# End of the first block's attention: a norm weight as a column, the pool mixer's two halves back to back, w_out's upper parts on ScalarE

## The chip, the cores and the metric

The kernel runs on one core of one Trainium2 chip. The metric is the device time of one execution in microseconds; below it is the median of the executions shown.

## What is computed

Two transformer blocks follow each other on 256 tokens of 1024 numbers, in float32. The change touches the end of the mixer of the first block. That mixer projects the normalized input and feeds three branches: a gated delta rule with 6 heads, an attention with compressed, selected and windowed keys, and a pool mixer that subtracts a token from running means over 2, 4, 8 and 16 tokens. The three outputs stand beside each other (384, 384 and 256 columns), and one product brings them back into the residual:

```python
o = gated_delta_rule(q, k, v, beta, g)
o = rms_norm(o, norm_g) * jax.nn.silu(heads(z))          # delta rule's output
mean = (cg[:, 1:] - cg_lag) / jnp.minimum(t1, float(w))  # pool mixer, per window w
outs.append(jnp.einsum('btc,cd->btd', mean - uf[..., sl], pool_w[gi]))
y = jnp.concatenate([y_a, y_b, y_c], axis=-1)
x = x + y @ w_out[l]
```

`norm_g` has 64 numbers, one for each place in a head, the same for all heads. After that come a feed-forward part, the second block with two attentions, and a layer of 32 experts, which this kernel goes through one after the other.

## The kernel before, in words

Activations stand in two layouts: tokens on the 128 partitions (two tiles `t` of 128 tokens) or channels on the partitions (`yT`, `xT`, 8 chunks of 128 channels by 256 tokens). For products in full precision each operand is split into an upper and a lower part, and three matmuls are made (`mm3`, L302 to L304; `mmc`, L404 to L406). A weight is split by `split` (L287 to 299): the upper part by an ACTIVATE on ScalarE (L297) or a TENSOR_SCALAR on GpSimd (L295), the lower part by a subtraction on VectorE (L298). With no engine named, `split` takes turns between ScalarE and GpSimd. There are three buffers for each part, so an upper part can be made only when the matmuls of the third one before it are done.

`block1` writes its steps as Python generators and calls them in the order of a string written out by hand, `ORDER1`. It sets the priority of every instruction. The order on each engine's queue is then made by a planner, which runs the program against its own costs of the instructions and issues what is ready in its model, by priority. On the chip each queue runs in that order, and an instruction that must wait holds up everything behind it on its engine.

The steps that matter here:

- `z` (`w_z`, L538 to 553) projects the gate z and applies silu to it, on token tiles. Its matmuls are the last that read `xT1`, whose two buffers `y_tiles` then hands to `yT`.
- `pm` (`pool_mix`, L667 to 697) has two halves `a`, and gives control back after each. For each it makes the running sums on GpSimd (L683 to 689), one pair of matmuls for each of two heads into a bank of PSUM (L693), and evicts the bank to the upper part of `yT` on ScalarE (L694) and the lower part on VectorE (L695).
- `rec` (`recur` and `out`) ends with the delta rule's output `y_a` of token tile t: sum with the last product (L1268), squares and their sum (L1270, L1272, L1273), the inverse root on GpSimd (L312, called with the name `rO`), and the product with it (L1276).
- `fin` (`finish`, L1278 to 1294) multiplies z by the norm weight on GpSimd (L1284), then y by z on VectorE (L1285), transposes y on TensorE in three pairs of heads (L1291, two PSUM banks in turn) and evicts each to `yT` (L1293 on ScalarE, L1294 on VectorE).
- `no` (`Nsa.out`, L898 to 944) makes the scores against the compressed keys (L910, L916), their softmax on VectorE and ScalarE (L921 to L929), transposes it (L933), evicts it (L935), multiplies with the values (L941), adds (L942) and writes chunks 3 to 5 of `yT` (L943, L944).
- `o` (`w_out`, L562 to 576) loads w_out, and multiplies for each half of the 1024 output columns the chunks of `yT` in the order 6, 7, 0, 1, 2, 3, 4, 5. Each chunk is one split and six matmuls (128x512). The loads go through SyncE's queue into a ring of six buffers of 1 MB.

The expert weights (some 200 MB) pass through the same queue and stream from HBM to the end of the program.

Of the kernel before, what the change touches and what calls it, by code (L numbers as in the profile page):

```python
# [9 lines left out]
F32 = mybir.dt.float32  # L10
# [3 lines left out]
AF = mybir.ActivationFunctionType  # L14
OP = mybir.AluOpType
# [3 lines left out]
P = 128  # L19
# [6 lines left out]
BK = dict(k="acc", v="acc", q="acc", nq="acc", ks="mg", kc="acc", u="mn", z="acc", a0="mn", a1="acc", a2="mn", a3="acc", a4="mn", a5="acc")  # L26
ORDER1 = ("nq k k gates k k nq gates k nq low v nq nq ks ks ks nq low kc ks ks low ks np v np v np v v v dbl "
# [3 lines left out]
SPL2 = dict(fq="p", fk="a", fv="g", dq="g", dk=None, dv=None, g0="g", g1="a", g2="g", g3="a", pa="a", pb=None, o0=None, o1=None, o2=None)  # L31
BK2 = dict(fq="acc", fk="acc", fv="acc", dq="acc", dk="acc", dv="acc", g0="acc", g1="acc", g2="acc", g3="acc")
ORDER2 = ("fk x x fq fk fk fk fk lam fq fq fv fq fq fq x fg fg fk fv fv fv fv fv dk f1 dk f1 f2 dk f1 dq f2 "
# [15 lines left out]
def _pack(items, dtype=np.float64):  # L49
    off, arrs, o = {}, [], 0  # L50
    for name, a in items:
        a = np.asarray(a, dtype).reshape(P, -1)
        off[name] = (o, a.shape[1])
        arrs.append(a)
        o += a.shape[1]
    return off, np.concatenate(arrs, axis=1)
# [52 lines left out]
def _params(I):  # L109

    def row(a):
        a = np.asarray(a).reshape(1, -1)
        return np.broadcast_to(a, (P, a.shape[1]))

    cw = I["conv_w"][0]
    first = [("g_mix", I["norm_mix"].reshape(8, P).T),
             ("cwT", cw.T.reshape(9, P, 4).transpose(1, 0, 2)),
             ("alog", row(I["a_log"])),
             ("dtb", row(I["dt_bias"])),
             ("wba", np.concatenate([I["w_in"][0][:, 1536:1548], I["w_in"][0][:, 2700:2718]], 1)  # L120
              .reshape(8, P, 30).transpose(1, 0, 2))]
    kn = I["nsa_k_norm"][0]
    rest = [("gng", row(I["gdn_norm"])),
            ("qcol", np.tile(I["nsa_q_norm"][0], 2)),
            ("kcol", np.tile(kn.T, (2, 1))),
            ("krow", row(kn[0])),
            ("posT", I["cmp_pos"][0].reshape(2, 16, 2, 64).transpose(2, 3, 0, 1)),
            ("w2c", I["cmp_w2"][0].reshape(2, 2, P, 64).transpose(2, 0, 1, 3)),
            ("pw", I["pool_w"][0].reshape(2, 2, 64, 64).transpose(1, 2, 0, 3)),
            ("psc", I["pool_scale"].reshape(2, P).T)]  # L130
    wr = np.concatenate([I["w_group_2"][0], I["w_expert_2"][0]], 1)
    dense = [("g_ffn", I["norm_ffn"].reshape(8, P).T)]
    block2 = [("g_mix2", I["g_mix_2"].reshape(8, P).T),
              ("bfg", row(I["b_fgate_2"])),
              ("lq", np.concatenate([row(I[n]) for n in ("lam_q1_2", "lam_q2_2", "lam_k1_2", "lam_k2_2")], 1)),
              ("gsub", I["g_subln_2"].reshape(P, 1)),
              ("wff", I["w_in_2"][0][:, 1536:1544].reshape(8, P, 8).transpose(1, 0, 2)),
              ("g_moeT", I["g_moe_2"].reshape(8, P).T),
              ("wr", wr.reshape(8, P, 36).transpose(1, 0, 2)),
              ("br", np.concatenate([row(I["b_group_2"]), row(I["b_expert_2"])], 1))]  # L140
    moe = [("g_moe", I["g_moe_2"].reshape(P, 8))]
    return [_pack(i, np.float32) for i in (first, rest, moe, block2, dense)]


_P1_SHAPES = (("g_mix", 8), ("cwT", 36), ("alog", 6), ("dtb", 6), ("wba", 240))
_P2_SHAPES = (("gng", 64), ("qcol", 1), ("kcol", 3), ("krow", 64), ("posT", 32), ("w2c", 256), ("pw", 128), ("psc", 2))
_P3_SHAPES = (("g_moe", 8),)
_P4_SHAPES = (("g_mix2", 8), ("bfg", 8), ("lq", 256), ("gsub", 1), ("wff", 64), ("g_moeT", 8), ("wr", 288), ("br", 36))
_P5_SHAPES = (("g_ffn", 8),)
# [287 lines left out]
def block1(K):  # L437
    nc, tc, I = K.nc, K.tc, K.I
    V, S, G, PE = K.V, K.S, K.G, K.PE
    C, CB, PR, idn, idb, mg, acc, dump = K.C, K.CB, K.PR, K.idn, K.idb, K.mg, K.acc, K.dump  # L440
    xt = K.xt
    with ExitStack() as st1:
        sp = K.sp
# [86 lines left out]
        z = wk.tile([P, 2, 384], F32, name="z")  # L530
# [22 lines left out]
        yT = []  # L553
# [6 lines left out]
        wo = []  # L560

        def w_out():  # L562
            for k in range(2):
                wo.append(load_out(K, I["w_out"][0][:, k * 512:k * 512 + 512], f"w_out{k}"))
                yield
            st1.close()
            K.early.close()
            s8b = K.st8.enter_context(tc.tile_pool(name="s8b", bufs=1, reuse_waits="tile"))
            K.s8b = lambda dt, name: s8b.tile([P, 8, T], dt, name=name, tag="s8b", bufs=2)
            K.xf = K.Rows(xt, PR("g_ffn"), "xTf", (K.s8b, K.s8b))  # L570
            for k in range(2):
                def ev(t, pv):
                    xs = xt[:, t, k * 512:k * 512 + 512]
                    V.tensor_tensor(xs, pv, xs, op=OP.add)
                yield from K.lin_tok(yT, wo[k], 512, sp, ev, order=(6, 7, 0, 1, 2, 3, 4, 5))
                K.xf.half(k)

        steps = dict(k=w_k(), v=w_v(), q=w_q(), nq=w_nq(), ks=w_ks(), kc=w_kc(), u=w_u(), z=w_z(), y=y_tiles(), o=w_out(),
# [1 line left out]
                     rec=g.recur(), fin=g.finish(z, yT), np=n.prep(few[:, :, 12:30]), cmp=n.compress(rbc),  # L580
                     no=n.out(yT), pm=pool_mix(K, wk, uT, yT))
# [365 lines left out]
def bc(ap, shape, axis):  # L947

    ix = [slice(None)] * len(ap.shape)
    ix.insert(axis, None)  # L950
    return ap[tuple(ix)].to_broadcast(list(shape))
# [13 lines left out]
class Gdn:  # L965
# [312 lines left out]
    def finish(self, z, yT):  # L1278
        K, wk, y = self.K, self.wk, self.y
        V, S, G, PE, mg, idn = K.V, K.S, K.G, K.PE, K.mg, K.idn  # L1280
        H = 6
        for t in range(2):
            zv = z[:, t].rearrange("p (h d) -> p h d", h=H)
            G.tensor_tensor(zv, zv, bc(K.PR("gng"), (P, H, 64), 1), op=OP.mult)  # L1284
            V.tensor_tensor(y[:, t], y[:, t], zv, op=OP.mult)  # L1285
            yield
        K.dump("y_a", y)
        for a in range(3):
            py = mg((P, 2, P), name="py")
            for t in range(2):  # L1290
                PE.transpose(py[:, t], y[:, t, 2 * a:2 * a + 2].rearrange("p a b -> p (a b)"), idn)  # L1291
            pf = py.rearrange("p a b -> p (a b)")
            S.activation(yT[0][:, a], pf, AF.Copy)  # L1293
            V.tensor_tensor(yT[1][:, a], pf, yT[0][:, a].bitcast(F32), op=OP.subtract)  # L1294


def attn_probs(K, wk, sc, off, nk, tag):
# [817 lines left out]
def device_arrays(inputs):  # L2115
    import ml_dtypes
    arrays = {f"in_{n}_dram": np.ascontiguousarray(inputs[n]) for n in _INS}
    arrays["in_c0_dram"] = _C0.astype(np.float32)
    arrays["in_cf_dram"] = _CF.astype(np.float32)
    arrays["in_cd_dram"] = _CD.astype(np.float32)  # L2120
    arrays["in_cb_dram"] = _CB.astype(ml_dtypes.bfloat16)
    arrays["in_cm_dram"] = _CM.astype(np.float32)
    arrays["in_cu_dram"] = _CU.astype(ml_dtypes.bfloat16)
    for n, (_, a) in zip(("p1", "p2", "p3", "p4", "p5"), _params(inputs)):
        arrays[f"in_{n}_dram"] = np.ascontiguousarray(a, np.float32)
    return arrays
# [15 lines left out]
```

## Time and profile before

| what | value |
| --- | --- |
| median of 3 runs | 1039.4 us (1038.61 to 1040.7) |
| the profiled execution | 1036.04 us, its span 1034.1 us |
| TensorE busy with matmuls | 989.6 us, 96% of the span |
| VectorE, ScalarE, GpSimd busy | 461.6, 277.3, 228.9 us |
| mean granted TensorE clock | 0.990 of full speed |

The span runs from the first to the last instruction in the profile; all times of a row are microseconds from its start. Matmuls are pipelined, so the profile's duration of one is longer than the distance to the next. PE is TensorE, DVE is VectorE, ACT is ScalarE, POOL is GpSimd, SP is SyncE. A row's bracket gives the time in which the engine stood idle before the instruction and what ended that wait.

### The profile page before, as it was taken

The numbers are of one execution on the slowest core, as the hardware profiler recorded it, in microseconds if no ns is written. First come the engines' busy times: TensorE is split into PE (matmuls) and PEld (weight loads), VectorE is DVE, ScalarE is ACT, GpSimd is POOL, SyncE is SP. The second block draws the span as 40 slices with busy tenths as digits, with TensorE's granted clock in tenths as the row PEclk, the third lists the DMA queues.
The fourth block names the chain that finished last, engine by engine and source line by source line (L and its number), as shares of the span: only waits on it lengthen the run. The fifth ranks groups of instructions, "written<-read, shape, count | busy, mean of one in ns | idle before, by whom it ended". The sixth has DMA issues, their size and how long they took to land. (4 is left out here: it accounts for less than half of the span.)

```text
span 1034.1 us, 16556 instructions
## 1 busy us (share of the span) xinstructions
PE 989.6 (96%) x6613; PEld 686.2 (66%) x6613; DVE 461.6 (45%) x948; ACT 277.3 (27%) x635; POOL 228.9 (22%) x318
## 2 busy tenths in 40 slices
PE   7999988999999999999999899999999999999995
PEld 6778766899988888887788434444444555555352
DVE  3878866665566653567688511111111111111012
ACT  3543333433333342435343011111101111111012
POOL 3682442222222225443337400000000000000000
PEclk9999997999999999999999999999999999999998
DMA  9552363755555554365677799999999999999994
GB/s 345 146 167 94 107 182 129 282 176 191 184 189 198 177 170 153 123 204 175 222 259 312 272 394 421 420 419 420 421 421 418 421 420 421 419 419 420 420 410 179
DMA packets 81999, 292.61 MB, mean 283 GB/s; under 512 B 11584, under 2 KB 26240, under 8 KB 58880
## 3 DMA queue, kind: packets, MB, share of 16 engines
q1 hardware_dynamic: 80768, 289.68, 73.9%
q10 hardware_dynamic: 1152, 1.86, 0.5%
q8 instruction: 53, 0.87, 0.3%
q14 instruction: 26, 0.21, 0.1%
HBM read 289.87 MB, written 1.64 MB: 282 GB/s over the span
## 5 line engine op out<-in xcount | busy, mean ns | idle before, releaser
L1802 PE MATMUL ph<-w,xe 128*64 128x512 f32 x1024 | 227.0, 593 | 2.3 <-DMA w<-in_w_dram 2.3
L1802 PEld LDWEIGHTS ph<-w,xe 128*64 128x64 f32 x1024 | 85.5, 137 | 132.5 <-issue 124.7
L1802 PE MATMUL po_e<-w,gT 128*64 128x512 f32 x528 | 115.1, 584 | 0.7 <-ACT gT L1911 0.7
L298 DVE TENSOR_TENSOR wl<-ffn,wh 128x512 fp32r<-128x512 f32 (+1 forms) x100 | 84.6, 849 | 62.4 <-ACT wh L297 31.3
L312 POOL TENSOR_TENSOR r<-r4a,mhalf 128x2 f32<-128x2 f32 x1 | 0.7, 698 | 442.1 <-DVE r4a L310 442.1
L1896 DVE COPY ws<-ppt 64x2 f32<-64x2 f32 x32 | 5.0, 157 | 194.8 <-ACT pT L1893 194.6
L1802 PEld LDWEIGHTS po_e<-w,gT 128*64 128x64 f32 x528 | 40.1, 136 | 63.8 <-issue 55.9
L295 POOL TENSOR_SCALAR wh<-ffn 128x512 fp32r<-128x512 f32 (+1 forms) x50 | 44.5, 890 | 138.3 <-PE acc_c L405 61.1
L405 PE MATMUL acc_c<-xTfl,wh 128*128 128x256 f32 x256 | 70.2, 283 | 0.0
L404 PE MATMUL acc_c<-xTfh,wh 128*128 128x256 f32 x256 | 70.1, 283 | 0.0
L1893 ACT ACTIVATE pT<-ppt 128x256 fp32r<-128x256 f32 x16 | 6.1, 384 | 225.4 <-PE ppt L1802 225.4
L406 PE MATMUL acc_c<-xTfh,wl 128*128 128x256 f32 x256 | 64.6, 283 | 0.0
L297 ACT ACTIVATE wh<-ffn 128x512 fp32r<-128x512 f32 (+1 forms) x50 | 37.4, 751 | 84.9 <-PE acc_c L405 42.2
L303 PE MATMUL acc<-wl,hh 128*128 128x512 f32 x128 | 50.8, 397 | 0.0
L304 PE MATMUL acc<-wh,hl 128*128 128x512 f32 x128 | 50.6, 395 | 0.0
L405 PEld LDWEIGHTS acc_c<-xTfl,wh 128*128 128x128 f32 x256 | 49.0, 192 | 0.5
L404 PEld LDWEIGHTS acc_c<-xTfh,wh 128*128 128x128 f32 x256 | 48.8, 192 | 0.4
L1802 PE MATMUL pgat<-ohb,xp 128*128 128x128 bf16 x768 | 48.4, 219 | 0.5 <-DVE ohb L1815 0.5
L1802 PEld LDWEIGHTS <-xp 128*128 128x128 bf16 x768 | 44.5, 98 | 6.3 <-issue 6.1
L406 PEld LDWEIGHTS acc_c<-xTfh,wl 128*128 128x128 f32 x256 | 45.6, 192 | 0.1
L303 PE MATMUL acc_t<-wl,xT2h 128*128 128x512 f32 x96 | 39.6, 412 | 1.5 <-DVE wl L298 1.5
L1830 DVE TENSOR_TENSOR xe<-pgat,p 128x512 f32<-128x512 f32 (+1 forms) x34 | 22.4, 660 | 36.6 <-PE pgat L1802 36.6
(743 smaller groups left out, 1995.5 us busy)
## 6 DMA issues: line engine op xcount, KB each, us to landing
w<-in_w_dram SPq DMA_DIRECT2D x180, 1024.0 KB, 19.8
ffn<-in_w_ffn_dram SPq DMA_DIRECT2D x32, 1024.0 KB, 5.3
w<-in_w_dram SPq DMA_DIRECT2D x22, 512.0 KB, 10.2
w_gate<-in_w_in_dram SPq DMA_DIRECT2D x8, 1024.0 KB, 5.1
cmp_w<-in_cmp_w_dram SPq DMA_DIRECT2D x4, 1024.0 KB, 5.5
w_o<-in_w_o_dram SPq DMA_DIRECT2D x4, 1024.0 KB, 5.1
w_in_ks<-in_w_in_dram SPq DMA_DIRECT2D x2, 1024.0 KB, 10.3
w_out<-in_w_out_dram SPq DMA_DIRECT2D x4, 512.0 KB, 4.1
```

Of the source, the lines that this page charges most:

```text
L295: G.tensor_scalar(hi, w32, 1.0, 1.0, op0=OP.mult, op1=OP.mult)
L297: S.activation(hi, w32, AF.Copy)
L298: (G if eng == "p" else V).tensor_tensor(lo, w32, hi.bitcast(F32), op=OP.subtract)
L303: PE.matmul(o, a[0], b[1], start=False, stop=False)
L304: PE.matmul(o, a[1], b[0], start=False, stop=stop)
L404: PE.matmul(o, a[0], b[0], start=start, stop=False, skip_group_check=True)
L405: PE.matmul(o, a[0], b[1], start=False, stop=False, skip_group_check=True)
L406: PE.matmul(o, a[1], b[0], start=False, stop=stop, skip_group_check=True)
L1802: last[0] = PE.matmul(*a, **k).ins
L1830: V.tensor_tensor(xe[:, c0:c0 + n], pg, bc(gmo[:, c0:c0 + n], (P, n, P), 2), op=OP.mult)
L1893: S.activation(pT, ppt[:, :2 * P].rearrange("p (t s) -> p t s", t=2), AF.Copy)
L1896: V.tensor_copy(ws[64 * g:64 * g + 64], ppt[64 * g:64 * g + 64, 2 * P + g:2 * P + 3:2 - g])
```

## The change

- The norm weight is no longer a row of 64 numbers on every partition, but a column with one number for each partition (two heads of 64 places). GpSimd's product with z goes away; the weight is the scale of the ScalarE eviction of each transpose, and VectorE's eviction becomes a product and subtraction in one instruction.
- In `ORDER1` the second `pm` stands directly behind the first, and the two later `pm` are gone.
- The splits of w_out name ScalarE for the upper part, all 16 of them.

```diff
-          "sco sol a1 sco sco a1 u kc rec z a2 cmp u u rec a1 a0 u u a2 a3 rec rec u a3 cmp rec a5 a2 y pm cmp "
-          "rec z z a5 prep z a3 z z cmp pm fin rec a5 no fin o pm fin no")
+          "sco sol a1 sco sco a1 u kc rec z a2 cmp u u rec a1 a0 u u a2 a3 rec rec u a3 cmp rec a5 a2 y pm pm cmp "
+          "rec z z a5 prep z a3 z z cmp fin rec a5 no fin o fin no")
...
-    rest = [("gng", row(I["gdn_norm"])),
+    rest = [("gng", np.tile(np.asarray(I["gdn_norm"]).reshape(-1), 2)),
...
-_P2_SHAPES = (("gng", 64), ("qcol", 1),
+_P2_SHAPES = (("gng", 1), ("qcol", 1),
...
-                yield from K.lin_tok(yT, wo[k], 512, sp, ev, order=(6, 7, 0, 1, 2, 3, 4, 5))
+                yield from K.lin_tok(yT, wo[k], 512, sp, ev, order=(6, 7, 0, 1, 2, 3, 4, 5), eng="a")
...
-            zv = z[:, t].rearrange("p (h d) -> p h d", h=H)
-            G.tensor_tensor(zv, zv, bc(K.PR("gng"), (P, H, 64), 1), op=OP.mult)
-            V.tensor_tensor(y[:, t], y[:, t], zv, op=OP.mult)
+            V.tensor_tensor(y[:, t], y[:, t], z[:, t].rearrange("p (h d) -> p h d", h=H), op=OP.mult)
...
-            S.activation(yT[0][:, a], pf, AF.Copy)
-            V.tensor_tensor(yT[1][:, a], pf, yT[0][:, a].bitcast(F32), op=OP.subtract)
+
+            S.activation(yT[0][:, a], pf, AF.Copy, scale=K.PR("gng"))
+            V.scalar_tensor_tensor(yT[1][:, a], pf, K.PR("gng"), yT[0][:, a].bitcast(F32), op0=OP.mult, op1=OP.subtract)
```

## Rows read from the trace of the kernel before

**Rows 1.** Windows: busy time of each engine, granted clock, DMA share, GB/s, two stretches.
```profile
150.00:175.00 25.00, 17.66 (x90) 12.38 (x86) 14.76 (x36) 4.89 (x13) 10.34 (x15) 0.73 0.13 46
...
700.00:800.00 100.00, 100.00 (x624) 46.75 (x622) 16.07 (x34) 11.48 (x22) 0.00 (x0) 1.00 1.01 420
```

**Rows 2.** Windows again, short ones, for the granted clock (third column from the right).
```profile
155.50:156.00 0.50, 0.00 (x0) 0.00 (x0) 0.50 (x2) 0.00 (x0) 0.50 (x1) 0.65 0.00 0
...
169.00:169.50 0.50, 0.50 (x3) 0.41 (x2) 0.01 (x1) 0.00 (x0) 0.46 (x1) 0.69 0.17 37
...
170.00:175.00 5.00, 3.09 (x25) 1.95 (x24) 3.10 (x7) 1.94 (x5) 1.20 (x2) 1.00 0.02 1
```

**Rows 3.** Timeline of TensorE's matmuls: start, duration, what, idle before and its releaser.
```profile
151.40 0.40 PE L303 MATMUL acc_t<-wl,yTh 128*128 128x512 f32 x1
151.63 0.40 PE L304 MATMUL acc_t<-wh,yTl 128*128 128x512 f32 x1
152.69 0.44 PE L1291 MATMUL py<-c,y_a 128*128 128x128 f32 x2 [0.66 <-DVE y_a L1285]
157.18 0.69 PE L1291 MATMUL py<-c,y_a 128*128 128x128 f32 x2 [4.05 <-DVE y_a L1285]
...
160.53 2.75 PE L916 MATMUL pcs<-kcT,qT 64*128 64x16 f32 x24
...
163.79 0.63 PE L303 MATMUL acc_t<-wl,yTh 128*128 128x512 f32 x1
164.22 0.63 PE L304 MATMUL acc_t<-wh,yTl 128*128 128x512 f32 x1
...
174.85 0.47 PE L302 MATMUL acc_t<-wh,yTh 128*128 128x512 f32 x1 [1.23 <-ACT yTh L943]
```

**Rows 4.** Timeline of VectorE: the product with the inverse root for the second token tile.
```profile
154.57 0.97 DVE L1276 TENSOR_TENSOR y_a<-y_a,rO 128x384 f32<-128x384 f32 x1 [1.45 <-POOL rO L312]
```

**Rows 5.** Tiles z, y_a and w_out: instructions, shortest/median/longest duration in ns.
```profile
L550 DVE SCALAR_TENSOR_TENSOR z<-zth,z x4: 345/351/760, 147.3 to 150.8; 128x192 f32<-128x192 f32 x4
...
L1284 POOL TENSOR_TENSOR z<-z,p x2: 1010/1126/1242, 148.4 to 151.2; 128x384 f32<-128x384 f32 x2
L1285 DVE TENSOR_TENSOR y_a<-y_a,z x2: 545/831/1117, 151.5 to 156.6; 128x384 f32<-128x384 f32 x2
...
L1276 DVE TENSOR_TENSOR y_a<-y_a,rO x2: 557/762/967, 130.0 to 154.6; 128x384 f32<-128x384 f32 x2
...
L298 DVE TENSOR_TENSOR wl<-w_out,wh x16: 681/693/1285, 143.7 to 188.0; 128x512 fp32r<-128x512 f32 x16
L297 ACT ACTIVATE wh<-w_out x8: 623/632/635, 143.0 to 185.8; 128x512 fp32r<-128x512 f32 x8
```

**Rows 6.** Tiles pyc and py: evictions with a column as scale, and without one.
```profile
L694 ACT ACTIVATE yTh<-pyc,p x2: 468/471/474, 145.8 to 160.4; 128x256 fp32r<-128x256 f32 x2
L695 DVE SCALAR_TENSOR_TENSOR yTl<-pyc,p,yTh x2: 479/481/483, 147.6 to 160.9; 128x256 fp32r<-128x256 f32 x2
...
L1293 ACT ACTIVATE yTh<-py x3: 378/384/384, 157.7 to 159.3; 128x256 fp32r<-128x256 f32 x3
```

**Rows 7.** GpSimd: busy with the second pool half (window, tile ps), then its timeline.
```profile
144.80:159.20 14.40, 6.52 (x10) 0.88 0.38 132
...
128.62 1.33 POOL L312 TENSOR_TENSOR rO<-ssO,mhalf 128x6 f32<-128x6 f32 x1
...
135.62 0.51 POOL L295 TENSOR_SCALAR wh<-w_in_z 128x384 fp32r<-128x384 f32 x1 [1.80 <-PE acc_t L304]
```

**Rows 8.** Timeline, all engines: first step of the compressed softmax, and its eviction.
```profile
163.30 0.26 DVE L921 TENSOR_REDUCE cnm<-pcs 128x6 f32<-128x96 f32 x1 [1.95 <-PE pcs L916]
...
167.97 0.26 DVE L929 TENSOR_TENSOR pc<-ce,cf 128x96 f32<-128x96 f32 x1
...
172.29 0.59 ACT L935 ACTIVATE pcTs<-pcT 96x512 f32<-96x512 f32 x1 [1.16 <-PE pcT L933]
```

**Rows 9.** Waits from 140 to 180 us: total, how often, the longest.
```profile
POOL wh L295 <- PE acc_t L304: 19.8, 4, 9.7
```

More of the change, by code (lines that the diff above doesn't have):

```diff
@@ L145 @@
 _P1_SHAPES = (("g_mix", 8), ("cwT", 36), ("alog", 6), ("dtb", 6), ("wba", 240))
-_P2_SHAPES = (("gng", 64), ("qcol", 1), ("kcol", 3), ("krow", 64), ("posT", 32), ("w2c", 256), ("pw", 128), ("psc", 2))
+_P2_SHAPES = (("gng", 1), ("qcol", 1), ("kcol", 3), ("krow", 64), ("posT", 32), ("w2c", 256), ("pw", 128), ("psc", 2))
 _P3_SHAPES = (("g_moe", 8),)
```

## The prediction
> **What bounds the kernel now.** The windows come first. From 700 to 800 us the DMA engines are full at 420 GB/s [rows 1]: the expert weights set the pace there, and no edit of the first block changes that pace. Their loads go through one queue and each waits for a buffer that earlier work frees, so I take it that the stream begins earlier by what the first block saves; if it began at a fixed time, the saving would be nothing. The stretch from 150 to 175 us is the other kind [rows 1]: TensorE works 17.66 of 25 us at a mean granted clock of 0.73, and no DMA is busy. There TensorE waits, 7.34 us in all, and pays for the wait a second time: the clock falls within 155.5 to 156.0 [rows 2], to half (1.2 of 2.4 GHz), and is back between 169.0 and 169.5.
>
> The timeline of TensorE shows why [rows 3]. The first six matmuls of w_out (chunk 6, the first pool half) end at 152.0. Then only two transposes are done, 0.44 us, until the second token tile of the delta rule's output comes at 157.18. The last 3.5 us before the clock fell held those 0.44 us of work and nothing else; 1.9 us of idle time between 170 and 175 [rows 2] brought no fall. Chunk 7 can't fill the hole, because the second pool half is still being summed on GpSimd. After the transposes come the compressed scores (160.53), then matmuls of w_out 0.43 us apart (163.79, 164.22) where they were 0.23 us apart before (151.40, 151.63). The first matmul that needs the attention's part of `yT` starts at 174.85, released by its eviction. That instant is what I compute anew.
>
> **The change part by part.** *The norm weight as a column* takes two products of 1.0 to 1.24 us from GpSimd (L1284) [rows 5]. They are off the direct chain, as the product with y comes later for other reasons. What they and the pool sums do is slow VectorE down: while GpSimd works, instructions with two operands in SBUF take longer. L298 takes up to 1.285 against 0.681 us, L1285 1.117 against 0.545, L1276 0.967 against 0.557, L550 up to 0.760 against 0.345 [rows 4, 5]. In the stage that ends at 157.18 stand two slow L298 (some 0.55 each, as an estimate between 0.51 and 0.60), one slow L1285 (0.57), one slow L1276 (0.41) and one slow L550 (0.41): 2.5 us. In return, the evictions get the column: ScalarE's go from 0.384 to the 0.471 us of L694, 0.09 each, three times; VectorE's to the 0.48 us of L695 [rows 6]. Both are in the times used below. The parameter's transfer becomes a little smaller, and no DMA is added or moved.
>
> *The pool halves back to back* move 6.52 us of sums on GpSimd [rows 7] out of the stretch from 144.8 to 159.2 to behind 129.95, where L312 ends. Nothing on SyncE's queue is passed, as the step issues no DMA; on GpSimd it passes the z gate's upper part at 135.62 [rows 7]. Two evictions then come when `yT` gets its buffers, so a second L695 (0.48) stands before y: net saving 2.5 - 0.5 = 2.0, and y is ready at 157.2 - 2.0 = 155.2. Chunk 7 fills six matmuls, 6 x 0.23 = 1.4 us, of the hole.
>
> *From y to the scores.* Two PSUM banks for three pairs: the third waits for the first's evictions, 0.47 + 0.48 us, and two times 0.3 us of transposes stand around it (an estimate from the 0.44 us of the pair at 152.69 [rows 3]): 1.55 us. If the planner keeps the order, the scores start at 156.7. They took 2.75 us at half clock; at the full one they take between 1.4 (half) and 2.75 (no gain). I take 1.6, because the large matmuls nearly halve, 0.43 to 0.23. They end at 158.3.
>
> *From the scores to chunk 3.* Before, this was 174.85 - 163.30 = 11.55 us [rows 3, 8]. The softmax takes 163.30 to 168.23, 4.93 us. Its transposes then stood behind slow matmuls of w_out. The eviction at 172.29 leads to 174.85 in 2.56 us. Without the slow clock I count 4.93 + 0.5 (transposes) + 2.56 = 8.0, and one more L298 in VectorE's queue, 0.69: chunk 3 starts at 158.3 + 8.0 + 0.7 = 167.0, which is 7.85 us earlier. The other ends: if the planner puts the scores into the hole in front of y, they can end at about 155.0 (152.0 + 1.4 for chunk 7 + 1.6), and chunk 3 starts at 155.0 + 8.7 = 163.7, a gain of 11.1; with scores that gain nothing it is 6.7. The check from the other side: half clock cost 14 matmuls x 0.20 = 2.8 us between 163.3 and 169.3 and some 1.6 on the scores and transposes, 4.4 together. So 17.66 - 4.4 = 13.3 us of work are left in a stretch of 25 - 7.85 = 17.15 us: 3.9 us of idle time remain, of 7.34.
>
> *w_out's upper parts on ScalarE.* Eight parts move from GpSimd to ScalarE at 0.63 us each (L297) [rows 5], 5.0 us in all. GpSimd waited long for its buffers here (19.8 us in four waits [rows 9]), so the part itself is not late; VectorE's L298 gains, with less GpSimd work beside it. The cover is ScalarE's idle time, 20 of 25 us [rows 1]. If that cover is missing, each part costs 0.63 where it stands in front of an eviction. Between nothing and 8 x 0.63 = 5.0 I take one, 0.6: three buffers are filled ahead, and seven of eight should lie in idle time.
>
> **Sum:** 7.85 - 0.6 = 7.2 us. Against the profiled execution, 1036.04 us (span 1034.1), that is 1028.8. That execution lies 3.4 us under the median of 1039.4, so for the median I forecast 1032.2.
>
> **Rivals.** *The clock falls all the same.* The 3.9 us of idle time that remain may lie in one piece, between the third chunk of y and chunk 3, when the attention's softmax is the last to come. For it: that much idle time is about what preceded the fall at 155.5. Against it: the pieces around y take some of it, and 1.9 us did no harm. It decides if most of the 3.9 us is one hole. Price: the 4.4 us of half clock again, so the gain is 2.8: 1036.6. Of the clock the Trainium skill says, in "TensorE: Matmul & The Clock Gate", section "HAM oscillation", that a kernel which lets the array wait between bursts pays the slow start after each such wait, not once; by that rule this rival is what happens, and the trace of before agrees at its first hole.
>
> *The pool sums come too late.* GpSimd has 135.6 - 129.95 = 5.7 us in front of the z gate's upper part, and the second half wants 6.5 [rows 7]. If it goes first, z is 0.8 us late, `yT` gets its buffers later by as much, and the hole stays open with the slow clock behind it: 7.2 - 0.8 - 4.4 = 2.0 us are left, 1037.4, just within what can be told from no change (0.2%, some 2.1 us). For it: the sums now have priority over z's last splits. Against it: TensorE has z's earlier chunks to work on meanwhile, and these sums ran beside a busy VectorE, so they may need less.
>
> *Slower: ScalarE's queue blocks.* On GpSimd one upper part waited 9.7 us for its buffer [rows 9], and nothing that others needed stood behind it. On ScalarE everything does: `yT`'s evictions and the softmax's exponentials. If the planner's model lets TensorE go faster through this stretch than the chip does, such a wait stands in front of an eviction, and the matmuls that would free the buffer come late too. The price is up to 9.7 us; it decides from 7.2 us on, where it eats the gain; in full the time is 1039.4 - 7.2 + 9.7 = 1041.9. Against it: ScalarE made half of the upper parts before, with shorter waits.
>
> **Numbers.** The forecast's chance is 0.48, the clock's 0.20, the pool sums' 0.15, the blocked queue's 0.17. The forecast's own range is 1028 to 1035. The range given, 1028.0 to 1040.5, takes in its best case (11.1 and no price on ScalarE), the clock and the pool sums, and leaves out most of the blocked queue. Faster by over 0.2%: 0.48 + 0.20 = 0.68; within 0.2%: 0.15; slower: 0.17.
>
> **What would show it.** Right: the pool half's second L693 stands before 145 us, chunk 7 follows chunk 6 directly, L1285 and L298 stay near 0.55 and 0.69 us, the granted clock is 1.00 from 150 to 170, and the first w_out matmul of chunk 3 stands near 167. Wrong, if the clock shows 0.5 after a hole before chunk 3 (first rival), if TensorE waits for `pmean` or z around 136 (second), or if the evictions L1293 and L935 wait on ScalarE behind L297 (third). The forecast is also wrong if the gain stands at 200 us and has gone by the time the expert weights stream.

## The result and the profile after

The changed kernel takes 1027.5 us (median of four executions, 1025.7 to 1029.63), the kernel before in the same set 1039.43 us: a ratio of 0.9885, with an interval of 0.9863 to 0.9907. That is 11.9 us faster; 1032.2 was forecast, with 1028.0 as the lower end. The profiled execution took 1025.7 us, its span is 1023.8 us. In the changed file the lines of `finish` stand two higher: L1283 is the product of y and z, L1289 the transposes, L1292 and L1293 the evictions.

The windows of the changed kernel, with the columns of [rows 1] and [rows 2]:

```profile
150.00:175.00 25.00, 23.36 (x143) 18.55 (x142) 19.41 (x52) 14.72 (x31) 1.32 (x2) 1.00 0.70 264
155.50:156.00 0.50, 0.50 (x4) 0.43 (x3) 0.34 (x2) 0.00 (x0) 0.00 (x0) 1.00 1.04 410
...
700.00:800.00 100.00, 100.00 (x621) 47.37 (x621) 17.43 (x36) 12.24 (x23) 0.00 (x0) 1.00 1.01 420
```

TensorE is busy for 23.36 of the 25 us where it was 17.66, the granted clock is 1.00 throughout, also in the half microsecond in which it fell before [rows 2], and the stage ends earlier. The stream of expert weights is as full as before, at 420 GB/s. The timeline of TensorE (start, duration, what, idle before and its releaser) shows the new order:

```profile
152.24 0.39 PE L304 MATMUL acc_t<-wh,yTl 128*128 128x512 f32 x1
152.47 0.60 PE L1289 MATMUL py<-c,y_a 128*128 128x128 f32 x4
153.00 0.24 PE L886 MATMUL pkt<-c,kc 32*128 32x32 f32 x1
...
154.08 1.51 PE L916 MATMUL pcs<-kcT,qT 64*128 64x16 f32 x24
155.53 0.50 PE L302 MATMUL acc_t<-wh,yTh 128*128 128x512 f32 x1
155.86 0.39 PE L303 MATMUL acc_t<-wl,yTh 128*128 128x512 f32 x1
156.10 0.38 PE L1289 MATMUL py<-c,y_a 128*128 128x128 f32 x2
...
160.05 0.72 PE L933 MATMUL pcT<-c,pc 128*96 128x128 f32 x4
161.47 0.68 PE L941 MATMUL poc<-pcTs,vcr 32*64 32x256 f32 x12 [0.70 <-ACT pcTs L935]
163.09 0.50 PE L302 MATMUL acc_t<-wh,yTh 128*128 128x512 f32 x1 [0.94 <-ACT yTh L943]
```

Chunk 3 starts at 163.09 where it started at 174.85 [rows 3]. Chunk 7 directly follows chunk 6, and the transposes follow it at 152.47. The compressed scores (L916) now stand **in front of** the third pair of transposes (156.10), and take 1.51 us instead of 2.75 [rows 3]. Of the 7.34 us of idle time two pieces are left in this stretch, 0.70 and 0.94 us.

The instructions that answer to [rows 5] and [rows 6], by tile (shortest/median/longest in ns):

```profile
L1283 DVE TENSOR_TENSOR y_a<-y_a,z x2: 537/545/553, 148.6 to 149.5; 128x384 f32<-128x384 f32 x2
L550 DVE SCALAR_TENSOR_TENSOR z<-zth,z x4: 351/353/354, 147.8 to 149.1; 128x192 f32<-128x192 f32 x4
L297 ACT ACTIVATE wh<-w_out x16: 630/632/642, 143.3 to 175.6; 128x512 fp32r<-128x512 f32 x16
L298 DVE TENSOR_TENSOR wl<-w_out,wh x16: 682/692/693, 144.0 to 176.3; 128x512 fp32r<-128x512 f32 x16
L1292 ACT ACTIVATE yTh<-py,p x3: 453/462/473, 153.2 to 156.5; 128x256 fp32r<-128x256 f32 x3
```

All the slow VectorE instructions of [rows 4] and [rows 5] are gone: no L298 over 0.693 us, no L1283 over 0.553. The product of y and z is done at 150.1 instead of 157.1, so y comes 7 us earlier, not 2. Part of that is this row, the sum with the delta rule's last product, whose two executions stood at 124.9 and 146.8 before:

```profile
L1268 DVE TENSOR_TENSOR y_a<-y_a,po x2: 555/555/555, 124.3 to 142.4; 128x384 f32<-128x384 f32 x2
```

**A yardstick.** The first L1268 stands between 124.3 and 126.1 in all the kernels below, and two profiles of the changed kernel differ by 1.0 us there. (In versions with added lines it is L1271 or L1285.) Counted from it, the same schedule gives the same distances: to chunk 3 it is 38.75 and 38.78 us in the two profiles of the changed kernel, and 49.94 before. So the gain is 11.2 us from the same start; the rest of 11.8 is a start that happened to be earlier. Where an experiment reorders the chunks, I take the distance to the first transposes of the next normalization (L329): 55.84 before, 44.68 and 44.72 after.

The saving passes down the kernel nearly whole: the eighth load of expert weights stands at 505.0 us instead of 516.9. Between it and the first expert's matmul, 1.6 us are lost again in this profiled execution (573.8 instead of 584.1), and the span is 10.3 us shorter. The place is a second hole on TensorE, behind the change: in both kernels it waits some 3.4 us for VectorE there. In this execution of the changed kernel the granted clock fell with it (0.82 from 565 to 570, 0.84 from 570 to 575), in that of the kernel before it stayed at 1.00, and six matmuls behind the hole take 2.91 us instead of 1.54. TensorE's timelines, the kernel before first:

```profile
580.51 0.20 PE L1744 MATMUL prk<-A,cu 128*128 128x64 bf16 x1 [3.38 <-DVE A L1739]
580.54 0.18 PE L1745 MATMUL prk<-A,cu 128*128 128x32 bf16 x1
580.57 1.54 PE L1717 MATMUL y<-xt,c 128*128 128x256 f32 x6
...
568.70 0.23 PE L1743 MATMUL prk<-A,cu 128*128 128x64 bf16 x1 [3.46 <-DVE A L1738]
568.74 0.21 PE L1744 MATMUL prk<-A,cu 128*128 128x32 bf16 x1
568.79 2.91 PE L1716 MATMUL y<-xt,c 128*128 128x256 f32 x6
```

The same schedule does both: in two executions of one other kernel (e6_norm_pool and r_no_act, below) these six matmuls took 2.91 and 1.54 us behind the same hole. Part of what separates executions of one kernel therefore arises behind the change, and a distance inside the stage tells more of the change than the total time.

### The profile page after: what moved, and what is told of

It reads as the page before. It is cut to its first block, busy times and chain, and to the rows that moved or that the text cites. A ratio compares the mean times of both kernels' runs of the same rounds, so it can differ in the third digit from the quotient of the medians.

```text
span 1023.8 us, 16550 instructions
## 1 busy us (share of the span) xinstructions
PE 984.8 (96%) x6613; PEld 683.4 (67%) x6613; DVE 458.3 (45%) x948; ACT 281.3 (27%) x643; POOL 220.1 (22%) x308
## 3 DMA queue, kind: packets, MB, share of 16 engines
HBM read 289.84 MB, written 1.64 MB: 285 GB/s over the span
## 5 line engine op out<-in xcount | busy, mean ns | idle before, releaser
L298 DVE TENSOR_TENSOR wl<-ffn,wh 128x512 fp32r<-128x512 f32 (+1 forms) x100 | 84.7, 850 | 62.4 <-ACT wh L297 31.4
L312 POOL TENSOR_TENSOR r<-r4a,mhalf 128x2 f32<-128x2 f32 x1 | 0.7, 696 | 442.2 <-DVE r4a L310 442.2
## 6 DMA issues: line engine op xcount, KB each, us to landing
w_in_ks<-in_w_in_dram SPq DMA_DIRECT2D x2, 1024.0 KB, 10.3
```

The source lines that it names most:

```text
L298: (G if eng == "p" else V).tensor_tensor(lo, w32, hi.bitcast(F32), op=OP.subtract)
```

## The experiments

Theory A: the gain comes from the order on TensorE that the two neighbouring pool halves let the planner find, with the delta rule's last products earlier. Theory B: it comes from GpSimd's relief of VectorE, which is my forecast's own reason. Theory C: the upper parts on ScalarE cost something. Theory D came later. All the runs in one table, in the order of their distance from the first L1268 to L329; each ratio is to the kernel before in the same set, whose median lies between 1038.3 and 1040.4 us:

| kernel | us to L329 | median, us | ratio to before, interval |
| --- | --- | --- | --- |
| e7_cmp_late | 56.04 | 1038.15 | 0.9982 (0.9967 to 0.9997) |
| before | 55.84 | 1039.4 | |
| e3_act: ScalarE part alone | 55.81 | 1039.5 | 0.9999 (0.9982 to 1.0016) |
| e9_warm | 52.61 | 1037.24 | 0.9984 (0.9964 to 1.0005) |
| e1_norm: column alone | 51.85 | 1035.75 | 0.9958 (0.9942 to 0.9975) |
| e13_bank | 50.37 | 1034.18 | 0.9963 (0.9944 to 0.9983) |
| e14_load | 48.84 | 1033.17 | 0.9927 (0.9901 to 0.9953) |
| e6_norm_pool | 47.44 | 1031.67 | 0.9944 (0.9925 to 0.9963) |
| e8_onebank | 46.36 | 1028.85 | 0.9909 (0.9882 to 0.9935) |
| e15_acc | 46.05 | 1029.91 | 0.9906 (0.9873 to 0.9939) |
| r_no_act, the kernel of e6_norm_pool | 45.91 | 1029.22 | 0.9906 (0.9886 to 0.9927) |
| e2_pool: halves alone | 45.85 | 1030.94 | 0.9910 (0.9893 to 0.9926) |
| e4_pool_act | 44.75 | 1028.11 | 0.9903 (0.9877 to 0.9929) |
| after, r_after | 44.68, 44.72 | 1027.5, 1027.8 | 0.9885, 0.9894 (0.9870 to 0.9918) |
| e11_fill | 43.46 | 1026.26 | 0.9875 (0.9854 to 0.9897) |
| e12_fill_g | 42.92 | 1025.93 | 0.9869 (0.9845 to 0.9893) |
| e15_mg | 42.33 | 1024.97 | 0.9871 (0.9841 to 0.9901) |

### The three parts alone

The column's lines alone, the two strings of `ORDER1` alone, and `eng="a"` alone, each on the kernel before.

> The norm weight as a column alone; the pool mixer's order and w_out's splits as before. Theory A (the order of the pool halves carries the gain, because it lets the planner put the delta rule's last products in front of the compressed branch's second half): the last product's sum L1268 stays near 146.8, the second pool half is still summed after 149, the hole on TensorE before the second token tile stays over 2 us, and the time is 0 to 3 us below before. Theory B (the gain is GpSimd's relief, each removed GpSimd instruction making VectorE faster): 3 to 5 us below before, with L1285 near 0.55 us both times.

> The pool halves back to back alone. Theory A: 8 to 11 us below before; L1268 near 142.4, the second L693 before 140, no fall of the clock between 150 and 170. Theory B: 3 to 5 us below before; L1268 stays near 146.8.

> w_out's upper parts on ScalarE alone. Theory A: within 1.5 us of before, the clock falls as before. Theory B: 2 to 3 us below before, as VectorE's slow lower parts (1.2 us) near 149 and 155 go to 0.7. Theory C, ScalarE's queue blocks: 1 to 3 us above before.

Measured: 4.3 us faster, 9.2 us faster, no difference. The first lies in theory B's range, the other two in theory A's, and theory C's loss is not there. The halves back to back carry 10.0 of the 11.2 us by the yardstick; the column alone carries 4.0, but the two together can't add up to more than the whole, so they overlap. In e2_pool, TensorE's timeline already has the order of the changed kernel:

```profile
155.11 1.51 PE L916 MATMUL pcs<-kcT,qT 64*128 64x16 f32 x24
156.89 0.38 PE L1291 MATMUL py<-c,y_a 128*128 128x128 f32 x2
...
162.19 0.42 PE L933 MATMUL pcT<-c,pc 128*96 128x128 f32 x2 [0.75 <-DVE pc L929]
163.30 0.68 PE L941 MATMUL poc<-pcTs,vcr 32*64 32x256 f32 x12 [0.68 <-ACT pcTs L935]
165.07 0.47 PE L302 MATMUL acc_t<-wh,yTh 128*128 128x512 f32 x1 [1.09 <-ACT yTh L943]
```

The scores go ahead of the third pair of transposes there too. Three holes stand in front of chunk 3, 2.52 us in all, where the changed kernel has two, 1.64 us in all.

### One part left out

```diff
# e4_pool_act: the changed kernel, the norm column undone
+            G.tensor_tensor(zv, zv, bc(K.PR("gng"), (P, H, 64), 1), op=OP.mult)
# e6_norm_pool, again as r_no_act: ScalarE's upper parts undone
-    ... order=(6, 7, 0, 1, 2, 3, 4, 5), eng="a")
+    ... order=(6, 7, 0, 1, 2, 3, 4, 5))
```

> The changed kernel without the norm column: GpSimd multiplies z by the weight as before (two products of 1.0 to 1.24 us). It gives what the column adds when the pool halves already stand back to back (alone, on top of the kernel before, it gave 4.3 us). If the two gains overlap because both end in the same limit (the compressed scores, which wait for the compressed keys at 153.5 and not for y): 1026.5 to 1029. If y is still what ends the wait (the pool halves alone had y times z at 152.8, 0.9 of it waiting for GpSimd's product): 1030 to 1032, 2 to 4 us above the changed kernel, with the scores at 155.1 and chunk 3 at 165.

> The changed kernel without ScalarE's upper parts: w_out's splits take turns between ScalarE and GpSimd as before. Alone that part gave nothing (1039.5 against 1040.1). If it gives nothing here either: 1026.5 to 1029. If GpSimd's upper parts (eight of 16) slow VectorE down in this now denser stretch, L298 takes 1.2 us instead of 0.69 where they meet, and chunk 3 comes 0.5 to 1.5 us later: 1028 to 1030. If ScalarE's evictions come sooner without them (the eviction that TensorE waits 1.12 us for at 148.6): 0.5 to 1 us faster than the changed kernel, 1026 to 1027.

> Once more the changed kernel without ScalarE's upper parts (w_out's splits take turns between ScalarE and GpSimd). Its first measurement was 4 us above what the column and the pool halves gave in the other runs, with executions between 1029.5 and 1034.1, and its profile shows 2.52 us of idle TensorE between 161.0 and 164.6, then a granted clock of 0.66 between 165 and 170. If ScalarE's upper parts are worth something only here, because without them the hole in front of chunk 3 is long enough for the clock to fall (my first rival, in a kernel where it can be seen): 3 to 5 us slower than the changed kernel in the same set, chunk 3 near 164.6, and again executions spread over more than 3 us. If that was a chance of the first run: within 1 us of the changed kernel.

> The changed kernel again, unaltered, as the yardstick for the others of this set. If the first measurement (ratio 0.9885, 0.9863 to 0.9907) was right: a ratio of 0.987 to 0.990 to the kernel before, the first w_out matmul of chunk 3 near 163.1 and the granted clock at 1.00 from 150 to 175.

Without the column nothing is lost: 44.75 against 44.70 us. Its 4 us in e1_norm were real, and the order of the halves takes them up. Without ScalarE's parts 1.2 us are lost (45.91), although the same part alone was worth nothing. The place is the softmax: from its start to chunk 3 it takes 8.4 us in e2_pool and e6_norm_pool, 7.5 in e4_pool_act and in the changed kernel. With GpSimd making upper parts, the two L929 took 0.57 and 0.55 us in e2_pool where 0.26 is usual, and TensorE waited 0.75 us for the second (row above); in e4_pool_act and the changed kernel neither happens.

r_no_act is the kernel of e6_norm_pool once more, and its instructions stand in the same order. Two windows of e6_norm_pool:

```profile
160.00:165.00 5.00, 2.48 (x22) 1.30 (x21) 4.67 (x13) 1.68 (x5) 1.30 (x2) 1.00 0.20 30
165.00:170.00 5.00, 5.00 (x17) 3.91 (x16) 3.19 (x7) 1.82 (x4) 0.62 (x1) 0.66 0.99 398
```

The same two of r_no_act:

```profile
160.00:165.00 5.00, 2.48 (x22) 1.30 (x21) 4.67 (x13) 1.68 (x4) 1.30 (x2) 1.00 0.17 25
165.00:170.00 5.00, 5.00 (x22) 4.05 (x23) 4.42 (x9) 2.67 (x6) 0.94 (x1) 1.00 0.96 384
```

After the same 2.52 us of idle time, in three pieces, the clock fell in one execution and not in the other, and the fall cost 47.44 - 45.91 = 1.53 us. This is my first rival; it exists, but as a matter of chance, at this length of hole. The medians fit no case well: 1031.67 is above all three cases of e6_norm_pool, and r_no_act lies 1.4 us above r_after, between its two.

### Where does the order come from?

```diff
# e7_cmp_late: the kernel before, the compressed branch's second part called later
-          ... y pm cmp rec z z a5 ...
+          ... y pm rec cmp z z a5 ...
# e8_onebank: the changed kernel, one PSUM bank for both pool halves
-        py = mn((P, T), name="pyc")
+        pyb = pyb if a else mn((P, 2, T), name="pyc"); py = pyb[:, a]
```

> Only one word of the order moves: the compressed branch's second half stands behind the delta rule's last step instead of in front of it; the pool's second half stays late, all else as before. Theory A has two halves, and this run tests the first: if it is the place of the delta rule's last products that counts, L1268 comes 2 to 5 us earlier and the time is 2 to 5 us below before, while the late pool half still leaves a hole. If only the pool's chunk 7 as a filler counts, L1268 may move but the time is within 1.5 us of before. Theory B: within 1 us of before.

> The changed kernel with one line different: the two halves of the pool mixer share one PSUM bank (two columns of 256 numbers in it) instead of asking for one each. Everything that the change computes stays, the halves stay back to back, and the order string is the same. Theory A (the gain that I had not forecast comes from the order of TensorE: the second half's bank stands in line in front of the compressed branch's banks, holds these back, and so the delta rule's last products move forward): with no second bank to wait for, the compressed branch goes first again, L1268 stands near 146.5 again instead of 142.4, y times z for the second token tile is done near 153.5 to 155.5 instead of 150.1, and the first matmul of chunk 3 stands at 165 to 167 instead of 163.1: 1029.5 to 1033 us, that is 2 to 5 us slower than the changed kernel and close to what I forecast, where the order was taken as kept. Theory B (the gain comes from GpSimd being free, and the order does not matter): 1026 to 1029, as the changed kernel, with L1268 anywhere.

e7_cmp_late changed nothing: the planner put TensorE's instructions in the order of the kernel before, so it says nothing on theory A. It is a second measurement of the kernel before, and its ratio of 0.9982 shows how far one can lie from 1 by itself.

In e8_onebank the order did change. The tag `mn` has three banks, and the program's order decides who gets the next one. With a bank of its own, the second pool half stands in that line in front of the compressed branch; without it, that branch (L855) directly follows the first half (L693) as before, and the delta rule's last product is late again, in TensorE's timeline of e8_onebank:

```profile
134.63 0.65 PE L693 MATMUL pyc<-pmean,p 64*64 64x256 f32 x4
135.21 1.07 PE L855 MATMUL phid<-cmp_w,F 128*32 128x256 f32 x16
...
145.40 1.43 PE L1267 MATMUL po<-U,DT 64*64 64x64 f32 x24
```

In the changed kernel L855 stands at 139.56 and L1267 begins at 138.41. Theory A's mechanism is real, but its price is 46.36 - 44.70 = 1.7 us at most, with a lower clock in e8's profile (0.75 between 155 and 160) inside it, and the median of 1028.85 lies in theory B's range, under theory A's. So it is not the main carrier either. In e8, too, the scores stand ahead of y's last transposes; they even begin before y is done, as VectorE's product with z and TensorE's scores in e8_onebank show:

```profile
154.24 0.56 DVE L1283 TENSOR_TENSOR y_a<-y_a,z 128x384 f32<-128x384 f32 x1
154.75 1.51 PE L916 MATMUL pcs<-kcT,qT 64*128 64x16 f32 x24
```

From the first L1268, y is ready after 28.8 us there, 32.2 before and 25.7 in the changed kernel: most of the gain is there with a late y. That led to **theory D**: in the kernel before, the scores could not go ahead of y, because the bank of the second pool half comes before theirs in the line, and its sums were late. [Rows 3] has the sequence, which I had read past: transposes at 157.18, and the scores at 160.53, with the pool half's matmuls between them.

```diff
# e13_bank: the kernel before, another set of banks for the second pool half
-        py = mn((P, T), name="pyc")
+        py = (K.mg if a else mn)((P, T), name="pyc")
# e14_load: e2_pool, and GpSimd makes the second half's sums again at the old place
-          ... z z cmp fin rec a5 ...
+          ... z z cmp pd fin rec a5 ...
```

> The kernel before with one line different: the second half of the pool mixer takes its PSUM bank from another set (tag mg, two banks) instead of the set mn (three banks) that is handed out in the order of the program. Its sums stay late on GpSimd and beside VectorE, chunk 7 stays behind them, the norm weight stays on GpSimd. Theory D (the compressed scores of the kernel before stood behind the second pool half, because its bank came before theirs in the line; taking it away lets them go ahead of y, and that is most of the gain of the pool halves): the scores and their softmax lie before y, from the first L1268 to the first w_out matmul of chunk 3 it takes 41 to 45 us instead of 48.6 to 49.9, and the time is 1031 to 1036. Theory B (GpSimd relief for VectorE and an early chunk 7 make the gain): nothing of that is changed, so 48 to 50 us and 1038.5 to 1041.

> The kernel with the pool halves back to back and nothing else of the change (e2_pool), and GpSimd does the second half's running sums a second time at their old place, from about 145 us on, into tiles that nobody reads. TensorE's order is that of e2_pool. It prices the work beside VectorE by itself. Theory B: the slow instructions of VectorE are back (L1276, L1285, L298 at 0.97 to 1.28 us), y comes 2 to 2.5 us later, and chunk 3 with it: 42 to 42.5 us from the first L1268 instead of 39.95, and 2 to 2.5 us more time than e2_pool. Theory D (the scores go ahead of y, and what ends the wait before chunk 3 is the compressed keys and the softmax): y comes later and the scores don't, 40 to 41 us, at most 1 us more than e2_pool.

One line, and no work saved, takes 5.5 us from the distance to L329 (50.37); chunk 3 starts 43.8 us from the first L1268, within theory D's 41 to 45. The median is 1034.18 against 1039.7 in that set; the interval of the ratio puts the gain at 1.8 to 5.8 us. The scores stand 11.5 us earlier from the same start, while the pool half waits for its sums as before. TensorE's timeline of e13_bank:

```profile
148.46 1.51 PE L916 MATMUL pcs<-kcT,qT 64*128 64x16 f32 x24
...
155.24 0.66 PE L933 MATMUL pcT<-c,pc 128*96 128x128 f32 x2 [2.66 <-DVE pc L929]
157.64 1.12 PE L693 MATMUL pyc<-pmean,p 64*64 64x256 f32 x4 [1.74 <-POOL pmean L689]
158.69 0.69 PE L1291 MATMUL py<-c,y_a 128*128 128x128 f32 x2
```

The hole in front of y is still there, and so is the slow clock (0.51 between 155 and 160). Theory D's mechanism is shown: the bank held the scores back. That it makes half of the gain of the pool halves is an estimate, for e13_bank is no clean release. The set mg also serves y's transposes, and the first pair now stands behind the pool half (158.69, last row), where the first token tile's transposes stood at 152.69 [rows 3]; and the scores stand 24.1 us from the first L1268, ahead of the 29.7 of the changed kernel. What remains of the 10.0 us, some 4.5, I put down to chunk 7 in the hole, to y's earlier coming and to the clock; these were not separated further.

In e14_load, theory D's numbers failed on the high side: 48.84 us, 3.0 more than e2_pool. The scores come only 0.9 us later than in e2_pool, counted from the same start (156.51 - 125.63 against 155.11 - 125.12). In the stretch where the rest was lost the clock is low, in two windows of e14_load:

```profile
155.00:160.00 5.00, 5.00 (x42) 4.41 (x43) 4.12 (x12) 1.21 (x4) 2.10 (x4) 0.74 0.21 50
160.00:165.00 5.00, 5.00 (x14) 3.90 (x14) 3.20 (x14) 0.92 (x2) 0.62 (x1) 0.58 0.39 161
```

Its executions lie between 1029.03 and 1034.16; at the lower end the load costs nothing, by e2_pool's 1030.94. Of the instructions that theory B named, the product with the inverse root was slow (0.96 us) and one L298 (1.20), the two products with z were not (0.55 each). Others were slowed that it did not name, on the way to the compressed keys, while GpSimd multiplied z (151.25 to 153.35). VectorE's timeline of e14_load:

```profile
151.50 0.97 DVE L887 SCALAR_TENSOR_TENSOR ht<-htt,hth 128x64 f32<-128x64 f32 x1
152.50 1.48 DVE L889 COPY hTv<-ht 128x90 f32<-128x90 f32 x2
```

The same steps take 0.20 and 0.30 us in e2_pool. So GpSimd's work beside VectorE is worth about 0.9 us here, and 2.1 more come with the fall of the clock; whether the load brought that fall or chance did, one profile doesn't show.

### The price of the clock

```diff
# e9_warm: the kernel before, five matmuls more behind the first transposes of y
+            pwm = K.acc((P, 384), name="pwarm") if t else None
+            for _ in range(5 * t):
+                PE.matmul(pwm, idn, z[:, 1], start=True, stop=True)
```

> The kernel before, with work added and nothing taken away: five float32 matmuls (128x384) whose result nobody reads, issued on TensorE between the transposes of the first and the second token tile of y, that is in the 4.05 us hole in front of 157.18. It measures the price of the half clock by itself. They take some 0.65 us each at full clock, 3.2 us together. If the fall of the clock costs what I worked out (4.4 us between 157 and 169.5): the granted clock stays at 1.00 from 150 to 170, the scores take about 1.5 us instead of 2.75, chunk 3 starts 3 to 4.5 us before 174.85, and the time is 1035 to 1037, although nothing was removed. If the idle time is all that counts and the clock nothing (the matmuls that run slowly stand beside waits for VectorE and ScalarE anyway): 1039 to 1040.5, with the clock at 1.00 all the same. If the dummy matmuls end too late, they hold the transposes at 157.18 back by up to 1 us, and that much is lost.

The planner put the six matmuls of chunk 6 behind the dummies (157.86), where the kernel before has them in front of y's transposes [rows 3]. So the hole in front of the dummies was still 2.34 us long, and the clock fell there (0.81 from 150 to 155, 0.85 to 160) instead of behind it. TensorE's timeline of e9_warm:

```profile
152.99 0.57 PE L1294 MATMUL py<-c,y_a 128*128 128x128 f32 x2 [2.34 <-DVE y_a L1288]
153.35 4.97 PE L1287 MATMUL pwarm<-z,c 128*128 128x384 f32 x10
...
160.63 1.51 PE L916 MATMUL pcs<-kcT,qT 64*128 64x16 f32 x24
```

From 160 on it was 1.00, the scores began as far from the start as before (35.5 against 35.6 us) and took 1.51 us, and chunk 3 came 3.5 us earlier by the yardstick, within the 3 to 4.5 expected: with more work, and nothing removed. As the order changed too, 3.5 us is the price of the clock only as far as the moved matmuls are worth nothing. The times don't settle it: they lie between 1031.98 and 1038.73, the median 1.1 us below the kernel before, and the interval holds no change.

### Versions that go on from there

```diff
# e11_fill: the changed kernel; one softmax for six heads, chunk 2 into the holes
-        V.tensor_reduce(nm, pss, axis=AX.X, op=OP.max)
+        for k in range(2):
+            V.tensor_reduce(nm[:, :, 3 * k:3 * k + 3], pcs[k], axis=AX.X, op=OP.max)
...
+                with tc.issue_after(b[t].ins) if b else ExitStack():
# e12_fill_g: and the third upper part of w_out on GpSimd
# e15_mg, e15_acc: and the second pool half's bank from mg, or from acc
```

> The changed kernel with the hole in front of chunk 3 filled. The softmax of the compressed scores runs once over all six heads instead of twice over three (the two maxima and subtractions stay apart, for the scores lie in two banks), so it takes some 3.1 us instead of 4.7; and the six matmuls of chunk 2 are queued behind the transposes of the probabilities (three) and behind the product with the values (three), where TensorE waited 0.70 and 0.94 us. If the end of the attention is what limits (theory A's next wait): chunk 3 starts 1.0 to 1.7 us earlier than 163.1, measured from the same start, the hole is under 0.6 us, and the time is 1.0 to 1.7 us below the changed kernel. If the limit is TensorE's work itself, because the matmuls of chunk 2 only change places: no gain. If chunk 2 is late because its lower part waits on VectorE: slower by up to 1 us.

> As the run before, and the upper part of w_out's third chunk is made on GpSimd instead of ScalarE, because at 146.5 it stands on ScalarE in front of the eviction of the window attention's probabilities, for which TensorE waits 1.12 us at 148.6. If ScalarE's queue makes that wait (the mechanism of my third rival, small): the wait shrinks by 0.5 to 0.6 us and the time by as much against the run before, 1.5 to 2.3 us below the changed kernel together. If GpSimd's work slows VectorE down there as much as it saves on ScalarE: no difference to the run before.

> The version with the filled holes (e12_fill_g, 1025.9 us, 37.0 us from the first L1268 to chunk 3) with the second pool half's bank from the set mg as well. The compressed branch no longer waits for that bank: in TensorE's planned order its second half stands before the delta rule's last products again, and half of the scores before the transposes of y. If the end of the softmax is what still ends the wait: 1 to 2 us less, 1024 to 1025.5. If the delta rule's later end (y as in the kernel before, some 4 us later) takes its place: 0.5 to 2.5 us more, 1026.5 to 1028.5. Theory A in its new form: both wait on TensorE's total work, there is less than 1.5 us of idle time left between 145 and 165, so no more than that can be gained.

> As the run before, with the bank from the set acc (three banks), which w_z's and w_out's sums use as well. TensorE's planned order has the whole compressed branch and the scores before the last window attention, and y late. If the scores' end limits: 1024 to 1025.5. If y limits, as it then comes last before chunk 0: 1026.5 to 1029, with TensorE idle in front of the transposes of the second token tile, and the clock may fall there.

e11_fill gains 1.25 us by the yardstick and 1.5 us in the median of its set, as expected of a hole that is filled. e12_fill_g halves the wait for the window attention's probabilities, in TensorE's timeline of e12_fill_g:

```profile
149.05 1.09 PE L815 MATMUL po<-PT,ksw 128*64 128x128 f32 x14 [0.61 <-ACT PT L807]
```

It was 1.13 us in e11_fill, and 0.54 us are gained. e15_mg has 0.6 us of idle time left between 145 and 165 and gains 0.6 more by the yardstick; its ratio is that of e12_fill_g. With 1024.97 us (1024.35 to 1027.01) it is the fastest version that ran, 2.5 us below the changed kernel by medians of different sets; the intervals of the two ratios overlap. e15_acc is slower, 46.05 us, but not as its second case had it: the median of 1029.91 is above that range, TensorE waits only 0.20 us in front of the second token tile, and the clock stays at 1.00 there.

## Why the prediction was wrong, point by point

**The scores: the step that failed.** I let the scores follow y (156.7), "if the planner keeps the order", and gave the other case, the scores in the hole in front of y, as the far end: chunk 3 at 163.7. That end is what happened. Counted from the start of the kernel before, the scores began at 154.08 + 0.57 = 154.65 and chunk 3 at 163.66. This is 2.05 us of the miss. I had the reason in [rows 3] without seeing it: it was not y that held the scores, but the bank of the second pool half, whose sums I described in the same paragraph. e13_bank shows it; and in e8_onebank the scores begin before y is done.

**Softmax to chunk 3.** I took 8.7 us; it took 7.46. The kernels with the halves back to back but without ScalarE's parts need 8.4, so my figure was nearly right for them, and some 1.0 of the difference of 1.24 us is what these parts brought.

**ScalarE's upper parts.** I charged 0.6 us. They cost nothing alone, and gained 1.2 us with the rest. VectorE's gain, which I named and did not price, was the larger side. A wait on ScalarE's queue did exist (1.12 us of TensorE at 148.6, halved by e12_fill_g), but it was not longer than in the kernels without them (1.38 us in e2_pool).

The sum: 2.05 + 1.24 + 0.6 = 3.9 of the 4.7 us by which the forecast was too high. The rest is within what executions of the changed kernel differ by (1025.54 to 1031.07 in ten), and part of such differences arises at the second hole, behind the change.

**y.** The chain on VectorE became 2.6 us shorter, from L1268 to the product with z, where I had 2.0. That it began 4.4 us earlier (3.9 from the same start) I had not foreseen (theory A), so my 155.2 for y was wrong as well. It was worth 1.7 us at most, as e8_onebank shows, since the scores no longer waited for y.

**Norm column.** Priced with the relief of GpSimd at 2.0 us together. The column is worth 4.0 us alone and nothing beside the pool halves. I had credited both to one chain, so the sum was not harmed.

**The clock.** 4.4 us for the half clock: e9_warm's chunk 3 came 3.5 us earlier, with a hole of 2.34 us left in it. It stayed at 1.00 as forecast, with 1.64 us of idle time left instead of 3.9. The first rival did not happen in the changed kernel, but did in e6_norm_pool. Of this the Trainium skill says, in "TensorE: Matmul & The Clock Gate", section "HAM oscillation", that a kernel whose waits between bursts are long enough pays the slow start again after each of them; here it did so after three waits of 2.52 us together in one execution and not in another of the same kernel.

**The other rivals.** The pool sums were not late: the second L693 stood at 139.0, and TensorE did not wait for it. The 5.7 us that I gave GpSimd for them were not all free, though: an L798 of 1.04 us stands in them, at 132.78. ScalarE's queue held no wait near 9.7 us; the upper parts waited like this, in the waits of the changed kernel from 140 to 180 us (total, how often, the longest):

```profile
ACT wh L297 <- PE acc_t L304: 8.0, 9, 2.0
```

## What to carry to other kernels

Before pricing a wait, look at what stands directly in front of the waiting instruction in its queue, and ask whether a buffer handed out in program order put it there: here one bank taken from another set moved the scores by 11.5 us and the end of the stage by 5.5 (e13_bank). Gains of parts that end in the same wait don't add up, and a part worth nothing alone can be worth something once that wait is gone, so try parts alone and left out. Measure distances from an event ahead of the change, not from the start of the trace.

## What the runs showed of the hardware

The granted clock is not decided by the schedule alone: the same instructions gave 0.66 and 1.00 in the same stretch (e6_norm_pool, r_no_act), 1.53 us apart, and the six matmuls behind the hole of some 3.4 us in front of the experts took 2.91 and 1.54 us in the same two executions. It also fell without a hole worth the name: in e8_onebank within 155 to 160, with 0.46 us of idle time, and in e14_load around 157, with 0.33 us since 151. In both the engine had just done the small matmuls of the compressed keys and scores (64x16, 32x32); the changed kernel does the same ones and kept 1.00. What tips it was not found.

What GpSimd costs beside VectorE depends on what it does at that moment: the two products of L1285, 1.12 and 0.55 us before [rows 5], took 0.55 each in e14_load, beside a GpSimd that ran L312 on a single column (154.01, 0.86 us). Nor are two operands in SBUF the condition, as I had put it: the copies of L889 have one, and took 0.64 and 0.91 us there against 0.19 in e2_pool.
